# RMSNorm with ReLU: loads and stores on two hardware DMA queues, twelve in-place f32 slots, gamma spread on chip

## The chip, the cores and the metric

The kernel runs on one core of a Trainium2 chip. The time is the device time of one execution in microseconds (us). The profile is one such execution; its span (first to last instruction) is about 2 us shorter than the time. TensorE is not used. ACT is ScalarE, DVE is VectorE, POOL is GpSimd, SP is SyncE; ACTq and SPq stand for the sequencer of an engine, which issues DMAs. SBUF and PSUM are the two on-chip memories that hold tiles here. The trace records for each DMA a completion semaphore, which rises when the DMA lands and for which others wait.

## The reference

x is 16 x 1024 x 512 in f32, so 16384 rows of 512; gamma is one row of 512. Every row is divided by its root mean square, multiplied by gamma, and clipped at zero.

```python
rms = np.sqrt(np.mean(x ** 2, axis=-1, keepdims=True) + eps)
x_norm = x / rms * gamma
return np.maximum(x_norm, 0).astype(np.float32)
```

33.55 MB come in and 33.55 MB go out. There are 128 rows for each of the 128 partitions; both kernels work in 16 chunks of 8 rows per partition, 2.1 MB each. Chunks, loads and stores are counted from 0 here.

## The kernel before

```python
x_tile, xg, o_tile        # pools with 4 buffers each; o_tile is bf16
# gamma: one DMA that reads the same 2 KB row for each of 128 partitions
gamma_bcast = bass.AP(tensor=gamma.tensor, offset=gamma.offset, ap=[[0, P], gamma.ap[0]])
nc.sync.dma_start(out=gamma_sbuf, in_=gamma_bcast)
... (cut)
for i in range(nchunks):
    nc.sync.dma_start(out=x_tile, in_=xv[:, s:s + K, :])              # load, hardware queue of SP
    nc.vector.tensor_mul(out=xg, in0=x_tile, in1=gammaK)              # 128 x 4096
    for j in range(K):                                                # squares and their sum
        nc.scalar.activation(out=sq_scratch, in_=x_tile[:, j, :], func=Square, accum_out=ss[:, j:j+1])
    nc.scalar.activation(out=rms, in_=ss, func=Sqrt, bias=eps_sbuf, scale=inv_d)
    nc.vector.reciprocal(out=rstd, in_=rms)
    for j in range(K):                                                # scale and clip, to bf16
        nc.vector.tensor_scalar(out=o_tile[:, j, :], in0=xg[:, j, :], scalar1=rstd[:, j:j+1],
                                scalar2=0.0, op0=mult, op1=max)
    nc.gpsimd.dma_start(out=ov[:, s:s + K, :], in_=o_tile)            # store, software queue, casts to f32
```

## Time and profile before

| | before |
|---|---|
| time, median of 3 runs | 165.87 us (165.78 to 166.01) |
| span of the profiled run | 164.0 us |
| busy: DVE, ACT | 122.8 us (75%), 99.4 us (61%) |
| bytes moved, mean rate | 67.40 MB, 411 GB/s |

These are lines of the page of the kernel before: the rows of 40 equal slices (a digit is the DMA engines' busy share in tenths), and two groups of instructions (count, busy us, mean ns of one, idle time of the engine before them and what ended it).

```profile
span 164.0 us, 565 instructions
DVE 122.8 (75%) x161; ACT 99.4 (61%) x274; POOL 8.9 (5%) x20
DMA  5999999999999999999999999999999999998994
GB/s 87 401 420 444 440 412 432 434 432 412 436 436 412 440 434 424 424 432 436 412 436 436 414 432 436 412 440 432 428 424 432 432 416 436 440 432 348 416 420 192
...
L74 ACT ACTIVATE sq_scratch<-x_tile 128x512 f32<-128x512 f32 x128 | 80.6, 630 | 48.8 <-DMA x_tile<-in_x_dram 45.3
L70 DVE TENSOR_TENSOR xg<-x_tile,gamma_sbuf 128x4096 f32<-128x4096 f32 x16 | 70.5, 4406 | 29.3 <-DMA x_tile<-in_x_dram 29.3
```

The DMA engines are hardly ever idle between the ends, and the two compute engines spend their idle time waiting for loads: the kernel is bound by DMA. So only the stretches where the rate lies under about 430 GB/s can be improved. The windows view shows them (start:end in us, then busy us of each engine with its instructions, granted clock, DMA share, GB/s; TensorE has none):

```profile
0.00:8.00 8.00, 0.06 (x1) 1.28 (x1) 0.20 (x4) 1.00 0.77 236
24.00:28.00 4.00, 3.09 (x2) 3.84 (x12) 0.67 (x1) 1.00 1.01 426
60.00:100.00 40.00, 33.65 (x49) 24.35 (x68) 2.53 (x5) 1.00 1.11 429
150.00:152.00 2.00, 1.97 (x6) 0.00 (x0) 0.53 (x1) 1.00 0.48 188
152.00:162.00 10.00, 2.15 (x6) 0.00 (x0) 0.53 (x1) 1.00 1.03 419
```

The first 8 us are poor (236 GB/s): gamma's 128 packets of 2 KB stand in front of x, their last part lands at 6.14 us and the first x tile at 11.01 us; the same view holds 150 to 152 us, a hole in which one store was nearly drained and the last was not computed. From the timeline of the kernel before, the first square and the last two stores (start, duration, what, in brackets the idle time before):

```profile
11.03 0.63 ACT L74 ACTIVATE sq_scratch<-x_tile 128x512 f32<-128x512 f32 x1 [9.01 <-DMA x_tile<-in_x_dram]
...
151.03 0.53 POOL L90 DMA_DIRECT2D out_dram<-o_tile  x1 [11.71 <-DVE rstd L80]
154.45 0.53 POOL L90 DMA_DIRECT2D out_dram<-o_tile  x1 [2.89 <-DVE o_tile L84]
```

### The profile page before, as it was taken

What the parts mean: (1) busy time and instruction counts of PE and PEld (TensorE: products, weight loads), DVE (VectorE), ACT (ScalarE), POOL (GpSimd) and SP (SyncE); (2) the same over time, 40 slices, a digit from 0 to 9 for tenths busy, and PEclk for the clock granted to TensorE, in tenths of its full rate; (3) what the DMA queues carried; (4) which work ended last, traced back from release to release, by engine and by line L of the source; (5) the groups of instructions that cost most, each with busy time, mean ns of one, the idle gap of its engine ahead of it and who ended that gap; (6) DMA issues with size and microseconds to landing.
All of it is one profiled execution on the core that took longest, in us unless ns stands there. A gap on an engine that the chain in (4) does not pass through costs nothing.

```text
span 164.0 us, 565 instructions
## 1 busy us (share of the span) xinstructions
DVE 122.8 (75%) x161; ACT 99.4 (61%) x274; POOL 8.9 (5%) x20
## 2 busy tenths in 40 slices
DVE  0029979999999999969498694968949498099600
ACT  3039999999993937739195682928649194094000
POOL 0000010011010101010100001010010101001100
DMA  5999999999999999999999999999999999998994
GB/s 87 401 420 444 440 412 432 434 432 412 436 436 412 440 434 424 424 432 436 412 436 436 414 432 436 412 440 432 428 424 432 432 416 436 440 432 348 416 420 192
DMA packets 4755, 67.40 MB, mean 411 GB/s; under 512 B 528, under 2 KB 528, under 8 KB 656
## 3 DMA queue, kind: packets, MB, share of 16 engines
q1 hardware_dynamic: 2448, 33.82, 57.4%
q0 software_dynamic: 2304, 33.56, 49.4%
q14 instruction: 3, 0.02, 0.0%
HBM read 33.82 MB, written 33.55 MB: 411 GB/s over the span
## 4 chain that ended last, share of the span: by engine, by line
issue 49%; DVE 27%; ACT 8%; DMA 6%; POOL 3%; POOLq 0%; SPq 0%
DVE xg L70 15%; DVE o_tile L84 11%; ACT sq_scratch L74 7%; DMA x_tile<-in_x_dram 6%; POOL out_dram L90 3%; ACT L77 1%; DVE rstd L80 1%; ACT rms L77 0%; POOLq L121 0%; SPq L48 0%; POOLq L90 0%
## 5 line engine op out<-in xcount | busy, mean ns | idle before, releaser
L74 ACT ACTIVATE sq_scratch<-x_tile 128x512 f32<-128x512 f32 x128 | 80.6, 630 | 48.8 <-DMA x_tile<-in_x_dram 45.3
L70 DVE TENSOR_TENSOR xg<-x_tile,gamma_sbuf 128x4096 f32<-128x4096 f32 x16 | 70.5, 4406 | 29.3 <-DMA x_tile<-in_x_dram 29.3
L84 DVE TENSOR_SCALAR o_tile<-xg,rstd 128x512 bf16<-128x512 f32 x128 | 52.1, 480 | 0.1
L74 ACT ACTIVATION_READ_ACCUMULATOR sq_scratch<-x_tile 128x1 f32 x128 | 23.9, 187 | 0.0
L90 POOL DMA_DIRECT2D out_dram<-o_tile x16 | 8.7, 541 | 145.9 <-DVE rstd L80 119.4
L77 ACT ACTIVATE rms<-ss,eps_sbuf 128x8 f32<-128x8 f32 x16 | 4.8, 301 | 0.5
L80 DVE RECIPROCAL rstd<-rms 128x8 f32<-128x8 f32 x16 | 3.1, 196 | 1.2 <-ACT rms L77 1.2
L74 ACT ACT_TABLE_LOAD x1 | 1.3, 1283 | 0.7 <-PEq L107 0.7
L77 ACT ACT_TABLE_LOAD x1 | 1.3, 1283 | 0.0
L51 DVE MEMSET eps_sbuf<- 128x1 f32 x1 | 0.1, 59 | 0.8 <-PEq L107 0.8
L107 POOL MEMSET const-float32-0.0<- 128x1 f32 x1 | 0.1, 99 | 0.2 <-issue 0.2
L107 POOL MEMSET const-bfloat16-1.0<- 128x1 bf16 x1 | 0.1, 102 | 0.0
L107 POOL MEMSET const-float32-1.0<- 128x1 f32 x1 | 0.1, 99 | 0.0
L107 POOL MEMSET const-uint8-127<- 128x1 uint8 x1 | 0.1, 99 | 0.0
## 6 DMA issues: line engine op xcount, KB each, us to landing
x_tile<-in_x_dram SPq DMA_DIRECT2D x16, 2048.0 KB, 26.4
out_dram<-o_tile POOLq DMA_DIRECT2D x16, 2048.0 KB, 21.3
gamma_sbuf<-in_gamma_dram SPq DMA_DIRECT2D x1, 256.0 KB, 5.4
```

What stands on the lines that cost most here:

```text
L51: nc.vector.memset(eps_sbuf, eps)
L70: nc.vector.tensor_mul(out=xg, in0=x_tile, in1=gammaK)
L74: nc.scalar.activation(out=sq_scratch, in_=x_tile[:, j, :], func=mybir.ActivationFunctionType.Square, accum_out=ssj)
L77: nc.scalar.activation(out=rms, in_=ss, func=mybir.ActivationFunctionType.Sqrt, bias=eps_sbuf, scale=inv_d)
L80: nc.vector.reciprocal(out=rstd, in_=rms)
L84: nc.vector.tensor_scalar(out=o_tile[:, j, :], in0=xg[:, j, :], scalar1=rj, scalar2=0.0, op0=mybir.AluOpType.mult, op1=mybir.AluOpType.max,)
L90: nc.gpsimd.dma_start(out=ov[:, s:s + K, :], in_=o_tile)
L107: nc = _bacc.Bacc("TRN2", target_bir_lowering=False, num_devices=1)
```

## The change

Its intent: keep the DMA engines full. Loads stay on SP's hardware queue and run up to twelve chunks ahead; stores go to ACT's hardware queue, in f32 and straight from the slot that the load filled, so that one slot serves load, compute and store. Gamma comes in as four rows of 2 KB and is spread over the partitions by one DVE shuffle, so that the first load of x is the first DMA. The scratch output of the squares moves to PSUM. Instructions keep the order of the program on each engine.

```diff
-    gamma_bcast = bass.AP(tensor=gamma.tensor, offset=gamma.offset, ap=[[0, P], gamma.ap[0]])
-    nc.sync.dma_start(out=gamma_sbuf, in_=gamma_bcast)
+    nc.vector.memset(gseed, 0.0)
+    for q in range(0, P, 32):
+        nc.scalar.dma_start(out=gseed[q:q + 1, :], in_=gamma[None, :])
+    nc.vector.stream_shuffle(gamma_sb, gseed, [0] * 32)
...
+    nslots = 12
+    slot = [slots.tile([P, K, d], F32, name=f"slot{s}") for s in range(nslots)]
+    junk = psum.tile([P, d], F32, name="junk")
+    ctx.enter_context(tc.manual_schedule())
+    def load(i):
+        nc.sync.dma_start(out=slot[i % nslots], in_=xv[:, i * K:(i + 1) * K, :])
+    def store(i):
+        nc.scalar.dma_start(out=ov[:, i * K:(i + 1) * K, :], in_=slot[i % nslots])
+    def compute(i):                       # cut: squares and root on ACT as before, then
+            nc.vector.tensor_mul(out=xt[:, a:b, :], in0=xt[:, a:b, :], in1=gammaG())   # in place
...
     for i in range(nchunks):
-        (load, product, squares, root, scaling to bf16, store by GpSimd)
+        load(i)
+        compute(i)
+        if i >= 1:
+            store(i - 1)
+    store(nchunks - 1)
```

On ACT, store i-1 comes after the squares of chunk i and before those of chunk i+1.

More of the change, by code (lines that the diff above doesn't have):

```diff
@@ L6 @@
 from concourse._compat import with_exitstack
+F32 = mybir.dt.float32
+ALU = mybir.AluOpType
+ACTF = mybir.ActivationFunctionType
 @with_exitstack
@@ L23 @@
     n, d = x2.shape
-    assert n % P == 0
-    rows_per_part = n // P
+    rows = n // P
     inv_d = 1.0 / d
@@ L31 @@
     K = 8
-    nchunks = rows_per_part // K
-    assert rows_per_part % K == 0
-    BF = mybir.dt.bfloat16
-    F32 = mybir.dt.float32
+    G = 8
+    nchunks = rows // K
+    nslots = 12
+    ngroups = K // G
     singles = ctx.enter_context(tc.tile_pool(name="singles", bufs=1))
-    pool = ctx.enter_context(tc.tile_pool(name="pool", bufs=4))
-    small = ctx.enter_context(tc.tile_pool(name="small", bufs=4))
-    gamma_sbuf = singles.tile([P, d], F32)
-    gamma_bcast = bass.AP(
-        tensor=gamma.tensor,
-        offset=gamma.offset,
-        ap=[[0, P], gamma.ap[0]],
-    )
@@ L48 @@
-    nc.sync.dma_start(out=gamma_sbuf, in_=gamma_bcast)
-    eps_sbuf = singles.tile([P, 1], F32)
-    nc.vector.memset(eps_sbuf, eps)
-    sq_scratch = singles.tile([P, d], F32)
-    gammaK = bass.AP(tensor=gamma_sbuf.tensor, offset=gamma_sbuf[:].offset,
-                     ap=[gamma_sbuf[:].ap[0], [0, K], gamma_sbuf[:].ap[1]])
-    for i in range(nchunks):
-        s = i * K
-        x_tile = pool.tile([P, K, d], F32)
-        nc.sync.dma_start(out=x_tile, in_=xv[:, s:s + K, :])
-        rstd = small.tile([P, K], F32)
-        rms = small.tile([P, K], F32)
-        ss = small.tile([P, K], F32)
-        xg = pool.tile([P, K, d], F32)
-        o_tile = pool.tile([P, K, d], BF)
-        nc.vector.tensor_mul(out=xg, in0=x_tile, in1=gammaK)
-        for j in range(K):
-            ssj = ss[:, j:j + 1]
-            nc.scalar.activation(out=sq_scratch, in_=x_tile[:, j, :],
-                                 func=mybir.ActivationFunctionType.Square,
-                                 accum_out=ssj)
-        nc.scalar.activation(out=rms, in_=ss,
-                             func=mybir.ActivationFunctionType.Sqrt,
-                             bias=eps_sbuf, scale=inv_d)
-        nc.vector.reciprocal(out=rstd, in_=rms)
-        for j in range(K):
-            rj = rstd[:, j:j + 1]
-            nc.vector.tensor_scalar(
-                out=o_tile[:, j, :], in0=xg[:, j, :],
-                scalar1=rj, scalar2=0.0,
-                op0=mybir.AluOpType.mult, op1=mybir.AluOpType.max,
-            )
-        nc.gpsimd.dma_start(out=ov[:, s:s + K, :], in_=o_tile)
@@ new lines @@
+    slots = ctx.enter_context(tc.tile_pool(name="slots", bufs=1))
+    small = ctx.enter_context(tc.tile_pool(name="small", bufs=1))
+    psum = ctx.enter_context(
+        tc.tile_pool(name="psum", bufs=1, space=bass.MemoryType.PSUM))
+    ctx.enter_context(tc.manual_schedule())
+    gseed = singles.tile([P, d], F32, name="gseed")
+    gamma_sb = singles.tile([P, d], F32, name="gamma_sb")
+    eps_sb = singles.tile([P, 1], F32, name="eps_sb")
+    junk = psum.tile([P, d], F32, name="junk")
+    slot = [slots.tile([P, K, d], F32, name=f"slot{s}") for s in range(nslots)]
@@ new lines, with gammaG @@
+    ss = [small.tile([P, K], F32, name=f"ss{i}") for i in range(nchunks)]
+    rms = [small.tile([P, K], F32, name=f"rms{i}") for i in range(nchunks)]
+    rstd = [small.tile([P, K], F32, name=f"rstd{i}") for i in range(nchunks)]
+    def load(i):
+        nc.sync.dma_start(out=slot[i % nslots], in_=xv[:, i * K:(i + 1) * K, :])
+    def store(i):
+        nc.scalar.dma_start(out=ov[:, i * K:(i + 1) * K, :], in_=slot[i % nslots])
+    def gammaG():
+        g = gamma_sb[:]
+        return bass.AP(tensor=g.tensor, offset=g.offset,
+                       ap=[g.ap[0], [0, G], g.ap[1]])
@@ new lines, in compute @@
+    def compute(i):
+        xt = slot[i % nslots]
+        for g in range(ngroups):
+            a, b = g * G, (g + 1) * G
+            for j in range(a, b):
+                nc.scalar.activation(out=junk, in_=xt[:, j, :], func=ACTF.Square,
+                                     accum_out=ss[i][:, j:j + 1])
+            nc.scalar.activation(out=rms[i][:, a:b], in_=ss[i][:, a:b],
+                                 func=ACTF.Sqrt, bias=eps_sb, scale=inv_d)
+            nc.vector.tensor_mul(out=xt[:, a:b, :], in0=xt[:, a:b, :], in1=gammaG())
+            nc.vector.reciprocal(out=rstd[i][:, a:b], in_=rms[i][:, a:b])
+            for j in range(a, b):
+                nc.vector.tensor_scalar(
+                    out=xt[:, j, :], in0=xt[:, j, :],
+                    scalar1=rstd[i][:, j:j + 1], scalar2=0.0,
+                    op0=ALU.mult, op1=ALU.max)
@@ L94 @@
+    nc.vector.memset(gseed, 0.0)
+    nc.vector.memset(eps_sb, eps)
+    for q in range(0, P, 32):
+        nc.scalar.dma_start(out=gseed[q:q + 1, :], in_=gamma[None, :])
+    nc.vector.stream_shuffle(gamma_sb, gseed, [0] * 32)
+    for i in range(nchunks):
+        load(i)
[3 more added lines that the diff above has]
+    store(nchunks - 1)
 _INS = ['x', 'gamma', 'eps']
```

## The prediction

> **What bounds the kernel now.** The DMA engines. The page's slices show DMA at 90% or more from the second to the last but one; DVE is busy 75%, ACT 61% of the 164.0 us span. 67.40 MB move; the windows view gives 424 to 436 GB/s in every stretch from 12 to 150 us, loads alone (12 to 20 us: 428) or shared with stores (80 to 100: 430). A load and a store of 2.1 MB together take about 9.8 us (landings in the trace), so one transfer takes 4.85 to 4.9 us. 32 of them need 155.4 to 156.5 us (estimate from those landings). The rest, about 8 us, lies at the two ends; only there is something to win.
>
> **Head.** Gamma is spread by a DMA of 128 packets of 2 KB, issued before the first x load. Windows of half a microsecond show 49 to 217 GB/s from 2.0 to 4.5 us instead of 430. Its last part lands at 6.1 us, and the first x tile lands 4.9 us later, at 11.0 us. The change replaces it by four rows of 2 KB on the other queue plus one shuffle on DVE (about 0.7 us, estimate: a plain DVE pass of 512 f32, from the 4.42 us that 4096 take), ready long before the first squares end. The first x load is then the first issue (about 0.7 us) and its data should start near 1.8 us. I expect the first x tile at 7 to 8 us. Gain: 2.5 to 3.5 us, all on the critical path.
>
> **Tail.** The last load lands at 143.3 us, the last two stores are issued at 151.0 and 154.4 us, and the windows view shows the DMA starving from 150 to 152 us (295 and 82 GB/s): about 1.1 us lost. With twelve slots, loads wait only for a store twelve chunks back. From the 4.9/9.8 us pace, I put the last load's landing at 136 us and the last store's issue at 150 us, with one or two stores still queued then: no starving. Gain about 1 us.
>
> **What it adds.** Multiplying by gamma in place makes DVE wait for the squares of the same chunk: 6.3 us of ACT, then 7.9 us of DVE (4.4 + 0.2 + 3.25), in series per chunk. But ACT meanwhile works on the next chunk, and 7.9 us is under the 9.8 us of a load and store. f32 instead of bf16 output should leave the 0.41 us pitch of the scaling steps. Store i-1 stands on ACT behind chunk i's squares: up to 2 us late near the end, covered by the backlog.
>
> **Two hardware queues** bring no bandwidth. [...] this trace agrees in that software stores beside hardware loads reach the same 428 to 430 GB/s as loads alone.
>
> **Sum.** Data from 1.8 us, [...] 32 x 4.87 = 155.8 us: last landing at about 158.1 (now 162.5), span about 159.6, and with the 1.9 us between span and time, 161.5 us. Range 159.5 to 164.2. The 2% line is 162.55. Chances: faster 0.68, within 2% 0.30, slower 0.02.
>
> **What would show it.** Right: near 430 GB/s from 2.5 us on; first x landing under 8 us; no dip before the last store; DVE total near 127 us; steady pace unchanged.
> **What would make it wrong.** Hardware-queue stores read 2.1 MB of SBUF instead of 1.05 and could run at another pace: 1% is 1.6 us. Store issues may block ACT. The head may ramp slowly without gamma too.

The sum came to a last landing at 158.1 us and a time of 161.5 us. Two terms of it stand above, 1.8 us and 155.8 us, together 157.6 us; a third, for the first packets, was a guess that no trace showed. The 1.8 us is in line with the trace of the kernel before, where the first DMA is issued at 0.74 us and its first packet starts at 1.75 us.

## The result, and the profile after

The changed kernel takes 165.74 us (median of 4 runs, 165.61 to 165.90), the kernel before 165.82 us in the same rounds. The ratio is 0.9995 (95% interval 0.9981 to 1.0010): no change. The prediction was 161.5 us, and the measured time lies outside its range.

The page of the changed kernel, the same lines:

```profile
span 163.5 us, 556 instructions
DVE 124.8 (76%) x164; ACT 99.8 (61%) x274; POOL 0.2 (0%) x4
DMA  5999999999999999999999999999999999999766
GB/s 208 430 425 433 433 405 353 429 427 441 429 427 425 437 437 425 433 433 429 425 441 429 433 425 431 441 421 437 429 429 429 429 441 433 421 437 425 301 256 257
...
L74 ACT ACTIVATE junk<-slot 128x512 f32<-128x512 f32 x128 | 77.0, 601 | 44.3 <-DMA slot<-in_x_dram 26.1
L78 DVE TENSOR_TENSOR slot<-slot,gamma_sb 128x4096 f32<-128x4096 f32 x16 | 70.7, 4419 | 21.5 <-ACT junk L74 21.5
```

The head is better (208 instead of 87 GB/s in the first slice), the end is worse (301, 256, 257). DVE now waits for ACT. A square, whose scratch output now goes to PSUM, takes 601 instead of 630 ns (0.03 us of 0.63; the squares make 4% of the chain of work that ended last). The windows view of the changed kernel:

```profile
0.00:8.00 8.00, 0.49 (x2) 1.28 (x1) 0.20 (x4) 1.00 0.79 316
24.00:28.00 4.00, 3.96 (x7) 3.84 (x11) 0.00 (x0) 1.00 0.95 324
60.00:100.00 40.00, 21.92 (x28) 17.32 (x49) 0.00 (x0) 1.00 1.01 430
154.00:157.00 3.00, 2.17 (x6) 0.00 (x0) 0.00 (x0) 1.00 0.05 22
157.00:162.00 5.00, 0.00 (x0) 0.00 (x0) 0.00 (x0) 1.00 0.99 419
```

Read against the five windows of before, in microseconds of transfer at 430 GB/s:

- By 8 us the kernel before has moved 1.63 MB of x (236 GB/s for 8 us, less 0.26 MB of gamma), the changed one 2.53 MB: 2.10 us gained.
- Between 28 and 140 us the changed kernel moves 0.33 MB more (431, 430 and 432 against 427, 429 and 428 GB/s in stretches of 32, 40 and 40 us): 0.76 us gained.
- From 24 to 28 us, where the first store sets in, there is a new dip, 324 against 426 GB/s: 0.95 us lost.
- The hole at the end has grown: 3 us at 22 GB/s (2.85 us) against 2 us at 188 GB/s (1.13 us): 1.72 us lost.

Together that is a gain of 0.2 us (2.10 + 0.76 - 0.95 - 1.72); the measured times differ by 0.1 us, the spans by 0.5 us. (Time less span is 1.7 to 1.9 us in the runs of the kernel before and 2.3 to 2.4 us in those of the changed one; where these 0.5 us go is not known.) So the gain was made and given back, most of it in the hole from 154 to 157 us, where the DMA engines had nothing left because the last store was issued at 156.2 us only. That store was late because DVE had stood still long before: from 60 to 100 us DVE is busy 21.92 us, against 33.65 us before, and from 100 us on it works without a break (39.82 of 40 us). The DMA was not short of work from 60 to 100 us; it ran at 430 GB/s, in part on loads that nobody needed yet (load 8 landed at 69.3 us, and ACT turned to it at 88.1 us). What DVE missed there is missing at the end.

Why did it stand still? ACT's timeline of the changed kernel (line L62 is the issue of a store, the records of the sums left out):

```profile
69.34 0.34 ACTq L62 DMA_DIRECT2D out_dram<-slot  x1
69.72 0.60 ACT L74 ACTIVATE junk<-slot 128x512 f32<-128x512 f32 x1 [10.09 <-DMA slot<-in_x_dram]
...
75.75 0.30 ACT L76 ACTIVATE rms<-ss,eps_sb 128x8 f32<-128x8 f32 x1
87.75 0.34 ACTq L62 DMA_DIRECT2D out_dram<-slot  x1
88.14 0.60 ACT L74 ACTIVATE junk<-slot 128x512 f32<-128x512 f32 x1 [12.09 <-DMA slot<-in_x_dram]
```

ACT stands still for 10 and 12 us, and each time the first thing that it does then is to issue a store. The view says that the squares waited for a load, and one would think of their own. The chain of waits of the changed kernel shows which load it was:

```profile
40.10 47.58 DMA slot<-in_x_dram
87.75 0.34 ACTq L62
```

The load issued at 40.10 us is load 10. It landed at 87.68 us, and at 87.75 us ACT issued store 6; then came the squares of chunk 8, whose data had landed at 69.3 us. Store 6 has no use for load 10. The waits of SP's queue show more such pairs (who waited for whom: us in all, times, longest):

```profile
SPq L59 <- DMA slot<-in_x_dram: 44.1, 5, 18.5
SPq L59 <- DMA out_dram<-slot: 22.2, 2, 14.5
SPq L59 <- DMA gseed<-in_gamma_dram: 6.2, 3, 3.6
```

Loads into fresh slots wait for rows of gamma, which they don't touch (6.2 us in three waits). What the pairs have in common is the completion semaphore: in the trace of the changed kernel load 4 raises the same one as a row of gamma, store 5 the same as load 8, store 6 as load 10, store 7 as load 11. And the later DMA of a pair is issued once the earlier has landed (store 7 was held by nothing but ACT's own work, which ended at 94.2 us):

| earlier DMA | lands, us | later DMA | issued, us |
|---|---|---|---|
| row of gamma | 6.32 | load 4 | 6.33 |
| load 8 | 69.26 | store 5 | 69.34 |
| load 10 | 87.68 | store 6 | 87.75 |
| load 11 | 93.81 | store 7 | 94.23 |

I read this as one wait: a DMA is held back until the one before it on its semaphore has landed. That is my reading of these pairs; how DMAs come by their semaphores no trace shows. Loads 8, 10 and 11 are two or three chunks further on than the chunk that ACT had just squared. In the trace of the kernel before, no store raises a semaphore that a load raises.

The wait for load 10 cost the DMA engines nothing (430 GB/s from 60 to 100 us), and ACT 12.09 us.

### The profile page after: what moved, and what is told of

Read it like the earlier page. It is cut to its first block, busy times and chain, and to the rows that moved or that the text cites. A ratio compares the mean times of both kernels' runs of the same rounds, so it can differ in the third digit from the quotient of the medians.

```text
span 163.5 us, 556 instructions
## 1 busy us (share of the span) xinstructions
DVE 124.8 (76%) x164; ACT 99.8 (61%) x274; POOL 0.2 (0%) x4
## 4 chain that ended last, share of the span: by engine, by line
DMA 52%; DVE 36%; ACT 4%; issue 2%; ACTq 1%; DVEq 0%
DMA slot<-in_x_dram 49%; DVE slot L78 21%; DVE slot L81 14%; ACT junk L74 4%; DMA gseed<-in_gamma_dram 3%; DVE rstd L79 1%; ACTq L89 0%; DVE gseed L86 0%; DVEq L128 0%; ACTq L62 0%; DVE eps_sb L87 0%
## 5 line engine op out<-in xcount | busy, mean ns | idle before, releaser
L74 ACT ACTIVATE junk<-slot 128x512 f32<-128x512 f32 x128 | 77.0, 601 | 44.3 <-DMA slot<-in_x_dram 26.1
L78 DVE TENSOR_TENSOR slot<-slot,gamma_sb 128x4096 f32<-128x4096 f32 x16 | 70.7, 4419 | 21.5 <-ACT junk L74 21.5
L81 DVE TENSOR_SCALAR slot<-slot,rstd 128x512 f32<-128x512 f32 x128 | 52.1, 481 | 0.6
L74 ACT ACTIVATION_READ_ACCUMULATOR junk<-slot 128x1 f32 x128 | 23.8, 186 | 0.0
L76 ACT ACTIVATE rms<-ss,eps_sb 128x8 f32<-128x8 f32 x16 | 4.8, 301 | 0.5
L86 DVE MEMSET gseed<- 128x512 f32 x1 | 0.5, 485 | 0.9 <-PEq L114 0.9
L91 DVE STREAM_SHUFFLE gamma_sb<-gseed 128x512 f32<-128x512 f32 x1 | 0.7, 724 | 0.0
```

The source lines that it names most:

```text
L74: nc.scalar.activation(out=junk, in_=xt[:, j, :], func=ACTF.Square, accum_out=ss[i][:, j:j + 1])
L76: nc.scalar.activation(out=rms[i][:, a:b], in_=ss[i][:, a:b], func=ACTF.Sqrt, bias=eps_sb, scale=inv_d)
L78: nc.vector.tensor_mul(out=xt[:, a:b, :], in0=xt[:, a:b, :], in1=gammaG())
L81: nc.vector.tensor_scalar(out=xt[:, j, :], in0=xt[:, j, :], scalar1=rstd[i][:, j:j + 1], scalar2=0.0, op0=ALU.mult, op1=ALU.max)
L86: nc.vector.memset(gseed, 0.0)
L91: nc.vector.stream_shuffle(gamma_sb, gseed, [0] * 32)
```

## The experiments

The theory, T: stores that share completion semaphores with far loads stop ACT in front of the squares it should do. Two rivals: R1, the multiplication in place ties DVE to the end of ACT's squares, and that chain is too slow; R2, twelve slots let the loads crowd out the stores. All kernels gave correct results. From the expectations below, clauses on which semaphore a DMA gets are cut (marked): no trace of those runs showed it. The time of the kernel before, run beside them, was 165.72 to 165.81 us (medians).

| run | edit | median us | ratio to before (95%) |
|---|---|---|---|
| changed kernel | | 165.74 | 0.9995 (0.9981 to 1.0010) |
| e1 | stores by GpSimd | 163.91 | 0.9889 (0.9873 to 0.9906) |
| e2 | 8 slots | 163.66 | 0.9874 (0.9859 to 0.9888) |
| e3 | 8 slots, product in its own buffer | 163.31 | 0.9857 (0.9843 to 0.9872) |
| e4 | kernel before, new gamma | 163.78 | 0.9881 (0.9866 to 0.9896) |
| e5 | three idle rows after load 12 | 171.76 | 1.0367 (1.0348 to 1.0387) |
| e6 | three idle rows after load 13 | 177.21 | 1.0697 (1.0679 to 1.0715) |
| e7 | e1 and a small early store | 164.08 | 0.9903 (0.9888 to 0.9917) |
| e8 | e1 and gamma as before | 165.62 | 0.9996 (0.9981 to 1.0011) |
| e9 | 6 slots | 163.71 | 0.9874 (0.9860 to 0.9888) |
| e10 | 10 slots | 165.56 | 0.9988 (0.9971 to 1.0005) |
| e11 | 6 slots, product in its own buffer | 163.36 | 0.9853 (0.9840 to 0.9866) |

### e1: stores by GpSimd

```diff
-        nc.scalar.dma_start(out=ov[:, i * K:(i + 1) * K, :], in_=slot[i % nslots])
+        nc.gpsimd.dma_start(out=ov[:, i * K:(i + 1) * K, :], in_=slot[i % nslots])
```

> The changed kernel with one edit: stores are issued by GpSimd (software queue) instead of ACT. Theory T (completion-semaphore sharing): [...] from the sixth store on a store waits for the landing of a load issued just before it that is 2 to 3 chunks further on than the compute, and this wait stands on ACT in front of the next squares. With software stores the waits are gone, ACT never waits over 2 us for a semaphore of a load that it does not need, DVE has no 10 us holes after 60 us, and the time is 161.9 to 163.3. Rival R1 (the in-place multiplication ties DVE behind ACT): unchanged, 165 to 166, holes stay. Rival R2 (twelve slots let loads crowd the stores out): unchanged, 165 to 166.

163.91 us, 1.8 us under the changed kernel; 0.6 us over the expected band, which the end of this document accounts for. Waits of the changed kernel, then of e1:

```profile
ACT junk L74 <- DMA slot<-in_x_dram: 26.1, 3, 12.1
DVE slot L78 <- ACT junk L74: 21.5, 3, 10.6
ACT junk L74 <- DVE slot L81: 14.5, 11, 1.7
```

```profile
ACT junk L74 <- DMA slot<-in_x_dram: 37.6, 11, 4.0
DVE slot L78 <- ACT junk L74: 16.2, 8, 3.5
```

The sum of ACT's waits for loads is even larger in e1 (37.6 against 26.1 us), but the longest is 4.0 and not 12.1 us: these are waits for the chunk that ACT needs next, in a kernel that the DMA paces. The hole before the last store is gone. The edit also takes the stores' short waits for DVE off ACT (14.5 us in all in the changed kernel); e9 below leaves these where they are. R2 falls: in e1 twelve loads were issued by 23 us, in the changed kernel nine, so the loads ran further ahead here and did no harm. R1 as the whole cause falls too, since the product is still in place.

### e2 and e3: 8 slots; 8 slots and a buffer for the product

```diff
-    nslots = 12
+    nslots = 8
# e3 also
+    xgs = [slots.tile([P, K, d], F32, name=f"xg{s}") for s in range(3)]
+        xg = xgs[i % 3]
... (cut)
-            nc.vector.tensor_mul(out=xt[:, a:b, :], in0=xt[:, a:b, :], in1=gammaG())
+            nc.vector.tensor_mul(out=xg[:, a:b, :], in0=xt[:, a:b, :], in1=gammaG())
... (cut)
-                    out=xt[:, j, :], in0=xt[:, j, :],
+                    out=xt[:, j, :], in0=xg[:, j, :],
```

> The changed kernel with 8 slots instead of 12. Loads run less far ahead[...]: a store now waits at most for a load two chunks further on. T: the long ACT waits shrink to a few us in all, 162.3 to 163.8. R1: 165 to 166. R2: part of the way, 163.5 to 165.

> 8 slots, and the product with gamma goes to one of three buffers of its own, so that it does not wait for the squares. T: within 0.5 us of the run with 8 slots. R1: at least 1.5 us faster than that run. Skeptical alternative: DVE starts earlier on a chunk at the tail by up to 6 us, which only helps if the DMA starves there.

163.66 and 163.31 us. Fewer slots are faster, and stores are again on ACT's hardware queue. What R1 blames costs 0.35 us, not 1.5 or more, with 8 slots (with 12, where ACT stands still for longer, it was not tried): e2 keeps a dip at the end (98 GB/s from 154 to 155 us) that e3 does not have. Long waits are not all gone in e2 (ACT 12.8 us at the longest, until a load landed, in front of the store issued at 79.86 us), but fewer follow each other, and DVE catches up (27.92 us busy from 60 to 100 us, against 21.92).

### e4 and e8: gamma alone, both ways

```diff
# e4, in the kernel before
-    nc.sync.dma_start(out=gamma_sbuf, in_=gamma_bcast)
+    nc.vector.memset(gseed, 0.0)
+    for q in range(0, P, 32):
+        nc.scalar.dma_start(out=gseed[q:q + 1, :], in_=gamma[None, :])
+    nc.vector.stream_shuffle(gamma_sbuf, gseed, [0] * 32)
# e8, in e1: the reverse of it
```

> The kernel before with gamma's spread alone changed (four rows by DMA, then a shuffle on DVE). The prediction's head term: first x tile lands at about 8 us instead of 11.0, and all of it shows in the time, 162.6 to 163.4. If the head's gain is taken back later (the first tile is not what the end waits for), 165 to 166.

> Software stores (12 slots) with gamma spread by the broadcast DMA as in the kernel before. First x tile at 11.0 us instead of 8.0. If all of the head's gain counts, 166.6 to 167. If 1 us of it is given back in the dip when the first store sets in (the kernel before, whose engines stand 1.9 us apart after gamma, shows no dip), the dip goes here and the time is 165.4 to 166.2.

In the kernel before, the new gamma saves 2.0 us (165.77 to 163.78 us); in e1, the old one costs 1.7 us (163.91 to 165.62 us). The first x tile lands at 8.1 us in e4 and 8.0 us in e1, against 11.0 us before and 10.7 us in e8, so the first tile gains 2.6 to 2.9 us and the time about 1 us less. The landing of a tile is that of its slowest engine (the sixteen parts of the first tile land from 9.09 to 11.01 us in the kernel before, from 7.27 to 8.04 us in the changed one); the bytes moved by 8 us, which count all sixteen, put the gain at 2.1 us (above). e4 was a little outside its band (162.6 to 163.4 us). Part of the difference is the dip at the first store.

The pair says more than it was made for. Gamma alone, with four x tiles and software stores as before, is as fast as the changed kernel freed of its long waits (163.78 us; e1, e2 and e9 take 163.66 to 163.91 us). The hole at the end is gone in e4 too, as its windows view shows:

```profile
150.00:152.00 2.00, 1.71 (x5) 0.00 (x0) 0.00 (x0) 1.00 1.03 418
```

And twelve slots, f32 stores and all the rest without the new gamma, which is e8, take the time of the kernel before (0.9996). So in these runs the gain comes from gamma: twelve slots added none to it (e8 against the kernel before), nor did the second hardware queue (e9 against e4). Only with a buffer of its own for the product (e3, e11) is the kernel some 0.4 us faster than e4.

Windows of e1 and of e8:

```profile
24.00:28.00 4.00, 3.96 (x7) 3.81 (x12) 0.00 (x0) 1.00 0.99 305
```

```profile
24.00:28.00 4.00, 4.00 (x3) 3.84 (x13) 0.67 (x1) 1.00 1.06 414
28.00:32.00 4.00, 3.96 (x10) 3.84 (x13) 0.00 (x0) 1.00 0.93 383
```

Against 430 GB/s, e1 loses 1.2 us there and e8 0.6 us ((16 + 47) x 4 / 430).

### e5 and e6: three idle rows

```diff
     for i in range(nchunks):
         load(i)
+        if i == 12:                # e6: 13; written out here, a table in the kernel; scr is a tile of its own
+            for r in range(3):
+                nc.sync.dma_start(out=scr[r:r + 1, :], in_=gamma[None, :])
```

> The changed kernel, still 12 slots and both hardware queues, with three extra DMAs of one 2 KB row each into a scratch tile, issued on SP right after load 12. They move nothing of use[...]. [...] no store waits for a load more than two chunks ahead of it. T: the ACT waits of 12 and 18 us go, 163.3 to 164.3. R2 (loads run too far ahead) and any theory by bytes, slots or queues: 165.5 to 166.

> The same three rows, one load later (after load 13). [...] T: ACT stands still from about 76 us until load 13 lands near 100 us, the chain of DVE work after it moves back, 168 to 175. Every rival: as the run before it, within 0.5 us.

171.76 and 177.21 us: 6 KB that nobody reads cost 6 and 11.5 us. My number for e5 was wrong by 8 us, and e6 ended 2 us over its band. In e5 I had counted the three rows as harmless, since they are small. But they stand in SP's queue behind load 12: it was issued at 60.12 us, the first row at 60.49 us, and the row that ended the wait landed at 101.41 us. The waits of e5 show it:

```profile
ACT junk L75 <- DMA scr<-in_gamma_dram: 18.8, 1, 18.8
ACT junk L75 <- DVE slot L82: 11.7, 9, 1.7
ACT junk L75 <- DMA out_dram<-slot: 10.8, 2, 7.4
```

The squares are put down as waiting 18.8 us for the row of gamma that was loaded into scratch: the row landed at 101.41 us, and the store in front of those squares was issued at 101.45 us. Nothing that computes touches that tile, so this wait is not one for data; that it is one for a shared semaphore is T's reading, and the profile infers it from semaphore events. In e6 ACT's longest wait, for the landing of a load, is 24.1 us. The rows also wait themselves, on SP, for loads (18.4 us in two waits in e5), and load 13 is issued at 89.3 us in e5 (60.0 us in the changed kernel). So the edits move loads as well as stores, though in e5 the DMA kept 431 GB/s from 60 to 100 us. With slots, queues and bytes (but for 6 KB) as they were, the three rows made the kernel 6 and 11.5 us slower; a version with twelve slots, both hardware queues and no long wait, which would be the cleanest test, I did not find.

### e9, e10 and e11: 6 slots, 10 slots, 6 slots and a buffer for the product

```diff
-    nslots = 12
+    nslots = 6                     # e10: 10; e11: 6, and the product as in e3
```

> The changed kernel with 6 slots. [...] T: no store waits on ACT for a load, no DVE hole over 4 us after 20 us, the DMA does not starve before the last store, 163.0 to 163.8. If the depth of the prefetch has a worth of its own, slower than with 8 slots (163.66).

> The changed kernel with 10 slots. [...] T: same holes, 165.3 to 166.0. R2 (the depth of prefetch itself crowds stores out): halfway between 8 and 12 slots, 164.4 to 164.9.

> 6 slots and three buffers of its own for the product with gamma, the candidate for the best version. Nothing waits on ACT for a far load and DVE need not wait for squares. The DMA bounds it; 162.8 to 163.6, at most 0.4 us from the run with 6 slots in place.

163.71, 165.56 and 163.36 us, each inside its band. With 10 slots ACT waits for loads as with 12 (26.0 us in three waits, the longest 11.9, against 26.1, three and 12.1), and the time is the same within 0.2 us; R2 wanted it halfway. With 6 slots ACT's longest wait for a load is 3.9 us, and the stillness goes. Waits and windows of e10, then of e9:

```profile
ACT junk L74 <- DMA slot<-in_x_dram: 26.0, 3, 11.9
...
60.00:100.00 40.00, 21.92 (x28) 17.40 (x49) 0.00 (x0) 1.00 1.01 432
154.00:157.00 3.00, 2.12 (x6) 0.00 (x0) 0.00 (x0) 1.00 0.08 33
```

```profile
ACT junk L74 <- DMA slot<-in_x_dram: 32.7, 10, 3.9
...
60.00:100.00 40.00, 35.05 (x43) 24.33 (x68) 0.00 (x0) 1.00 1.00 429
154.00:157.00 3.00, 0.00 (x0) 0.00 (x0) 0.00 (x0) 1.00 1.01 431
```

The DMA moves the same from 60 to 100 us in both, DVE works 13 us more in e9, and at 154 us the DMA has a backlog in e9 and nothing in e10. The number of slots acts in these runs through the long waits that come with it, not through the depth of the prefetch: 6 slots do as well as 8. e11 and e3 beat both kernels, by 1.5% and 1.4%.

### e7: is the dip at the first store a cold start?

```diff
+    nc.gpsimd.dma_start(out=ov[:, 0, 0:128], in_=gseed[:, 0:128])   # 64 KB, written again by store 0
     nc.vector.stream_shuffle(gamma_sb, gseed, [0] * 32)
```

> Software stores (12 slots) with a small store of 64 KB issued at about 10 us, long before the first real one, to rows that are written again later. The run without it shows a dip of the DMA to 305 GB/s from 24 to 28 us, when the first store sets in: about 1.1 us of transfer lost. If the dip comes from the first use of the store queue or of the output memory, it goes and the time falls to 162.6 to 163.2; if not, 163.6 to 164.1.

164.08 us, no gain. The small store was issued at 10.40 us, and the dip is as it was:

```profile
24.00:28.00 4.00, 3.96 (x6) 3.81 (x13) 0.00 (x0) 1.00 0.97 297
```

So the first use of the store queue or of the output is not what makes it. In the same window it is 1.2 us in e1 and 0.4 us in e4 (new gamma, twelve slots and four x tiles), and from 24 to 32 us 0.6 us in e8 (twelve slots, old gamma); the kernel before (four x tiles, old gamma) has none (426 GB/s). So in these runs it is larger with twelve slots than with four x tiles, and with the new gamma than with the old; its cause stays open.

## Why the prediction was wrong

- **Bound by DMA, something to win only at the two ends: right.** The pace stayed at about 430 GB/s, and hardware stores in f32 run no slower than software stores from bf16 (430 against 429 GB/s from 60 to 100 us).
- **Head, "2.5 to 3.5 us, all on the critical path": mechanism right, size off.** Alone it is worth 1.7 us (e8) to 2.0 us (e4). The term was read from the landing of the first tile, its slowest engine.
- **The start of the first tile: mis-sized.** In the sum the first tile lands 31 transfers of 4.87 us before the last landing of 158.1 us, at 7.13 us; it lands at 8.04 us, 0.9 us later.
- **"covered by the backlog", and "no starving": this is the step that failed.** I looked at what stands behind what on ACT and counted only the wait of a store for its own DVE work. I took it that "loads wait only for a store twelve chunks back", and never asked what else a store could wait for. The runs showed stores that wait for far loads (12.09 us for store 6), DVE idle for 18 of the 40 us from 60 to 100 us, and 2.85 us of starved DMA before the last store. Taking the waits away (e1, e9) brings 1.8 and 2.0 us. "Gain about 1 us" at the tail thus became a loss of 1.72 us. The prediction did name "Store issues may block ACT" among its risks, without a number for it.
- **A dip at the first store: missing from the sum.** It takes 0.8 to 1.2 us in the runs with 6 to 12 slots and the new gamma.
- **"Two hardware queues bring no bandwidth": right, but not the whole.** The rate from 60 to 100 us was 430 GB/s with two, and 429 GB/s with one and a software queue. But the stores on the second queue shared completion semaphores with loads (store 6 with load 10), and stood on an engine that computes: ACT waited 12.09 us.

With the failed step mended, the sum's last landing of 158.1 us becomes 158.1 + 0.9 (first tile) + 0.8 to 1.2 (dip) = 159.8 to 160.2 us. This is an account after the fact. The last store of e1 lands at 160.4 us, and the last packets of e9 and e11 end at 160.2 to 160.3 us, so the rest of the sum holds to within a microsecond. Without the far waits the change is worth 1.1 to 1.5% (e1, e3, e9, e11), still under the 2% that was forecast, and gamma alone brings 1.2% (e4).

## What to carry to other kernels

In this program DMAs waited for things that have nothing to do with their data (store 6 for load 10, 12.09 us on ACT). When you put stores and loads on queues of the same kind, list from the trace what the issue of each DMA waited for, and ask where that stands in its queue. Issue stores from an engine that has nothing else to do, because a blocked issue holds up whatever stands behind it (stores by ACT 165.74 us, by GpSimd 163.91 us); and prefer the shallowest prefetch that keeps the DMA full (6 slots, 163.71 us, did what 12, 165.74 us, could not). Try the parts of a change alone: here the new gamma by itself (e4) was worth as much as the mended whole (e1, e9), within 0.15 us. When a DMA-bound kernel starves at its end, look for the engine that stood still much earlier, while the DMA was still busy with loads nobody needed.

## What else was measured

- Between the issue of a DMA and its first packet: 1.0 us for the first load of the changed kernel (issued at 0.73 us, first packet at 1.72 us). With loads in flight it was longer: store 0 was issued at 21.95 us, and its first packet started at 26.19 us.
- The dip when stores set in beside a stream of loads: 297 (e7) to 340 GB/s (e9) from 24 to 28 us in the runs with gamma spread on chip and 6 to 12 slots whose window was read, instead of 430, that is 0.8 to 1.2 us.
- A broadcast load of one row: 256 KB as 128 reads of the same 2 KB took 5.4 us from issue to landing in the kernel before (its first packet came 1.0 us after the issue), and the 2.1 MB load behind it landed 4.9 us after it. Whether the small packets or the one row make it slow was not tested.
